# Top-256 selection: thresholds found by probing with false position and taking the eight largest of the rest, with the bitwise search kept behind a branch

## The chip, the cores and the metric

The kernel runs on one core of a Trainium2 chip. The core has a matrix engine (TensorE, PE in the profile), a vector engine (VectorE, DVE), a scalar engine (ScalarE, ACT), GpSimd (POOL) and a queue engine that issues the DMA transfers (SyncE, SP). Each works through its own instruction stream in order. The metric is the device time of one execution in microseconds (us); lower is better.

## The reference

Two transformer blocks run on a sequence of 2048 tokens of width 1024. The first block has two kinds of attention. The second projects its input, picks 256 keys for every query by an index score, attends to these alone, runs a gated recurrence (HGRN) beside it, and projects the sum. What the change touches is the picking:

```python
s_h = relu(einsum('bqhd,bkd->bqhk', qib, ki_r) * IDX_DIM**-0.5)     # 4 index heads
s_idx = einsum('bqhk,bqh->bqk', s_h, wib)
s_idx = where(key_pos[None, :] <= q_pos[:, None], s_idx, -inf)      # causal
_, sel = lax.top_k(s_idx, 256)                                      # per query row
# attention over the meta tokens and c_r[sel] only
```

So every query row needs the set of its 256 largest scores, ties going to the lowest key. Rows 0 to 255 have at most 256 keys and need no search. The other 1792 rows are 14 tiles of 128 rows; tile i (2 to 15) has 128(i+1) columns, 133 column blocks of 128 in all.

## The kernel before

The kernel is written with a scheduler that orders each engine's instructions ahead of time from priorities (the place in the program, moved by `high_priority`) and a model of durations; a loop in the source is unrolled, and work of later lines can be put into the gaps of earlier lines.

The program is `phase_first` (block one), `phase_proj2` (the projections of block two, index scores and selection) and `phase_dsa` (attention, HGRN, output). The change is in `phase_proj2` and behind `phase_dsa`.

In `phase_proj2`, `Index.scores` (L1457 to L1481) computes the scores of a tile: PE multiplies (L1469, L1470), ACT and DVE apply ReLU and the head weights (L1473 to L1477), POOL adds two halves (L1478), and SP stores the f32 scores to `d_sc`. `lat` computes latent keys and values. `stream` (L291) then runs twelve projection blocks: each loads 256 columns of weights, ACT, DVE and POOL scale and split them in two f16 halves (`load_w`, L255 to L277), and PE multiplies in three passes (`mm3_T`, L319 to L321, 512 columns an instruction; `mm3_R`, L330 to L332, 256 columns). ACT, and for some blocks DVE or POOL, takes the results out of PSUM, which gives PE its next bank.

`select` (L1500) finds for each row the 256th largest score as a 32-bit key, one bit a step, for a batch of tiles at once. It runs four times: tiles 2 to 7 beside 8 and 9 (pools `tk` and `ty`), and tiles 10 to 12 beside 13 to 15 (`tk` and `tk2`). Each of the 32 steps counts how many scores of each row lie at or above a candidate. `share` (L1484) splits a tile's columns for that: ACT counts some by a Sign with an accumulated sum on the f32 scores (L1553), DVE the others by a compare with an accumulated sum on 16-bit halves of the scores (L1545). About eight operations on one column per tile (L1538, L1539, L1577 to L1583) then set the next candidate. After the search each tile is turned into a mask of 0 and -1e30 (L1607 to L1623: Sign on ACT, a compare, a running count L1616 and a select L1620 on DVE, a subtraction on POOL, L1622 on DVE) and stored to `d_mask`, which `phase_dsa` reads. The mask stage of the second pair has its priority lowered by 800 (`LATE`).

Of the kernel before, what the change touches and what calls it, by code (L numbers as in the profile page):

```python
# [2 lines left out]

# [6 lines left out]
F32 = mybir.dt.float32  # L10
F32R = mybir.dt.float32r
BF = mybir.dt.bfloat16
F16 = mybir.dt.float16
I32 = mybir.dt.int32
U16 = mybir.dt.uint16
AF = mybir.ActivationFunctionType
ALU = mybir.AluOpType
AX = mybir.AxisListType
PSUM = bass.MemoryType.PSUM
DRAM = bass.MemoryType.DRAM  # L20

S = 2048
# [11 lines left out]
LATE = -800  # L34
# [39 lines left out]
PC, PO, NA, Z2 = -200, -1500, 5, 1  # L74
ACAP, DCAP = 9, 12
LEVELS = (1, 2, 4, 8, 16, 32, 64)
BATCHES = [((2, 3, 4, 5, 6, 7), (8, 9)), ((10, 11, 12), (13, 14, 15))]


def ap(t, off, pat):  # L80
# [1154 lines left out]
def phase_proj2(K, A, E, finish):  # L1235
    nc, tc = K.nc, K.tc
    K.wbufs, K.rbufs, K.wpool = 6, 4, WPOOL[1]
    with ExitStack() as st:
# [171 lines left out]
        finish(ps, "pp")  # L1410
        wp = st.enter_context(tc.tile_pool(name="w2", bufs=2, reuse_waits="tile"))
        tk = st.enter_context(tc.tile_pool(name="tk", bufs=1, reuse_waits="tile"))
        sy = st.enter_context(ExitStack())
        ty = sy.enter_context(tc.tile_pool(name="ty", bufs=1, reuse_waits="tile"))
        for g in range(NG):
            if g > 1:
                idx(g)
# [13 lines left out]
        blocks = [(*w2_of(A, cols), K.xinv, set2(kind, cols[0][0]), kind in ("ga", "gh")) for kind, cols in BLK2]  # L1431

        stream(K, wp, pst, [*blocks[:4], lambda: wo_scale(K, wp, pst, A["w_out_2"], "st"), *blocks[4:10], lambda: rel_rows(K, A, sp, pt, "pt0"), *blocks[10:]], "st")
        (x0, y0), (x1, y1) = BATCHES
        select(K, tk, x0, [x0, x1], 0)
        select(K, ty, y0, [y0], 0)
        sy.close()
        tk2 = st.enter_context(tc.tile_pool(name="tk2", bufs=1, side="right", reuse_waits="tile"))
        select(K, tk, x1, [x0, x1], LATE)
        select(K, tk2, y1, [y1], LATE)  # L1440
        with tc.high_priority(offset=-300):
            prod_scale(K, sp, pt, bd[:, :2], K.zm, K.as_, K.ainv, "pt0")

# [37 lines left out]
            nc.sync.dma_start(K.d_sc[i * 128:(i + 1) * 128, u * 512:u * 512 + w], acc)  # L1481


def share(tiles):  # L1484

    def parts(x):
        r = []
        for i in tiles:
            a = min(max(x, i + 1 - DCAP), i + 1, ACAP)
            r.append((a, i + 1 - a))  # L1490
            x -= a
        return r

    def cost(r):
        return max(sum(w * p[k] + f * (p[k] > 0) for p in r) for k, (w, f) in enumerate(COUNT))

    return min((parts(x) for x in range(sum(tiles) + len(tiles))), key=cost)


def select(K, tk, tiles, batches, late):  # L1500
# [105 lines left out]
    with K.tc.high_priority(offset=late):  # L1606
        for n, i in enumerate(tiles):  # L1607
            w = 128 * (i + 1)

            sn = junk("ja", w)  # L1610
            eq = junk("jd", w)
            pr = hflat[:, :w].bitcast(F16)
            c = cn[:, n:n + 1]
            nc.scalar.activation(sn, sc[n], AF.Sign, scale=-1.0, bias=fc[:, n:n + 1], accum_out=sg[:, n:n + 1])
            nc.vector.tensor_scalar(eq, sn, 0.0, None, op0=ALU.is_equal)
            nc.vector.tensor_tensor_scan(pr, eq, eq, 0.0, op0=ALU.add, op1=ALU.max)  # L1616

            nc.vector.tensor_tensor(c, sg[:, n:n + 1], pr[:, w - 1:w], op=ALU.add)
            nc.vector.tensor_scalar(c, c, 0.5, 256.0 - w / 2, op0=ALU.mult, op1=ALU.add)
            nc.vector.scalar_tensor_tensor(eq, pr, c, eq, op0=ALU.is_le, op1=ALU.mult)  # L1620
            nc.gpsimd.tensor_tensor(sn, sn, eq, op=ALU.subtract)
            nc.vector.tensor_scalar(sn, sn, -0.5, NEG, op0=ALU.is_gt, op1=ALU.mult)  # L1622
            nc.sync.dma_start(K.d_mask[i * 128:(i + 1) * 128, :w], sn)  # L1623


class Hgrn:
# [414 lines left out]
def build(tc, A, out):  # L2041
    nc = tc.nc
    with ExitStack() as ctx:
        K = Ctx()
        K.nc, K.tc, K.ctx = nc, tc, ctx
        consts(K)
        dp = ctx.enter_context(tc.tile_pool(name="dram", bufs=1, space=DRAM))
        for name, shape, dt in (
                ("d_q", [512, 2, S], F16), ("d_k", [512, 2, S], F16), ("d_kx", [8, 5, S], F16), ("d_qx", [1, 5, 512], F16),
                ("d_kc", [1, 2, NK], F16), ("d_z", [S, D], F32), ("d_qb", [512, 2, S], F16), ("d_kb", [128, 2, S], F16),  # L2050
                ("d_vf", [10, 128, NT, 129], F16),
                ("d_o", [S, D], F32), ("d_x1", [S, D], F32), ("d_qi", [256, 2, S], F16), ("d_ki", [64, 2, S], F16),
                ("d_q2", [512, 2, S], F16), ("d_k2", [512, 2, NK], F16),
                ("d_vf2", [8, 128, NT + 1, 129], F16), ("d_z2", [S, D], F32), ("d_f", [512, NK], F32),
                ("d_qh", [512, S], F32), ("d_i", [NK, 512], F32), ("d_sc", [S, S], F32), ("d_mask", [S, S], BF),
                ("d_rb", [2, 8, 512], F32), ("d_rbb", [8, 512], BF), ("d_cs", [2, 128, S], F32), ("d_gg", [1, D], F32), ("d_a", [S, D], F32)):
            setattr(K, name, dp.tile(shape, dt, name=name))
        with ExitStack() as sk:
            phase_proj2(K, A, *phase_first(K, A, sk))
        phase_dsa(K, A, out)  # L2060


def layout(i):
# [38 lines left out]
    for m in LEVELS:  # L2102
# [2 lines left out]
        s_ = np.arange(128)[:, None]  # L2105
        lv.append((s_ // (2 * m) == t // (2 * m)) & (s_ % (2 * m) < m))
    A["lvl"] = f(np.stack(lv, 1).astype(np.int32))
    p = np.arange(128)
    A["cum_l"] = ((p[:, None] % 8 == p[None, :] % 8) & (p[:, None] < p[None, :])).astype(np.float32)
    A["inv_freq"] = f(np.tile((10000.0 ** (-np.arange(32) / 32.0)).astype(np.float32), 4)[:, None])  # L2110
# [16 lines left out]
```

## Time and profile before

| | |
|---|---|
| time, median of 3 runs | 3434.53 us (3431.0 to 3434.55) |
| profiled execution | 3434.66 us; its span, first to last instruction, 3432.9 us |
| mean granted clock of TensorE | 0.915 of full |
| busy, share of span | PE 88%, DVE 72%, ACT 54%, POOL 41% |
| selection (first load of scores to last mask store) | 1496 to 2424 us of the span |

A profile is one execution. Busy time counts an engine's instructions and no waits; matmuls overlap in it, so a busy PE still has gaps. The trace can be asked for the busy time of each engine in a stretch, for groups of instructions by source line, for who waited for whom, and for instructions in order of time. A group's line gives the count, the busy time, the mean of one in ns, and behind the bar the idle time before them with what ended it.

### The profile page before, as it was taken

The numbers are of one execution on the slowest core, as the hardware profiler recorded it, in microseconds if no ns is written. First come the engines' busy times: TensorE is split into PE (matmuls) and PEld (weight loads), VectorE is DVE, ScalarE is ACT, GpSimd is POOL, SyncE is SP. The second block draws the span as 40 slices with busy tenths as digits, with TensorE's granted clock in tenths as the row PEclk, the third lists the DMA queues.
The fourth block names the chain that finished last, engine by engine and source line by source line (L and its number), as shares of the span: only waits on it lengthen the run. The fifth ranks groups of instructions, "written<-read, shape, count | busy, mean of one in ns | idle before, by whom it ended". The sixth has DMA issues, their size and how long they took to land. (4 is left out here: it accounts for less than half of the span.)

```text
span 3432.9 us, 67228 instructions
## 1 busy us (share of the span) xinstructions
PE 3006.7 (88%) x25150; PEld 1864.1 (54%) x25150; DVE 2480.9 (72%) x6097; ACT 1857.6 (54%) x3512; POOL 1415.0 (41%) x1235
## 2 busy tenths in 40 slices
PE   7899999999978998998878878787878898988997
PEld 5555444678844555443345753256555566555664
DVE  7423865666676766479999999995677778776654
ACT  4424755665565556345555576652555555555663
POOL 3212466643235454222233313122455556565653
PEclk9999999999968999998899888898678898999999
DMA  6332435322243432333234411113553443333332
GB/s 229 85 90 73 135 107 169 103 84 70 89 152 119 139 119 90 102 126 84 78 81 116 149 53 56 56 56 101 152 144 99 129 124 96 99 110 90 92 92 72
DMA packets 264288, 361.14 MB, mean 105 GB/s; under 512 B 55228, under 2 KB 185136, under 8 KB 262808
## 3 DMA queue, kind: packets, MB, share of 16 engines
q1 hardware_dynamic: 263528, 356.82, 34.5%
q8 instruction: 197, 3.23, 0.4%
q14 instruction: 131, 1.07, 0.1%
q10 hardware_dynamic: 432, 0.02, 0.0%
HBM read 243.92 MB, written 112.82 MB: 104 GB/s over the span
## 5 line engine op out<-in xcount | busy, mean ns | idle before, releaser
L746 POOL TENSOR_TENSOR plo<-p,phi 128x512 f16<-128x512 f32 (+4 forms) x628 | 680.4, 1095 | 710.7 <-ACT phi L742 444.9
L742 ACT CAST phi<-p 128x512 f16<-128x512 f32 (+4 forms) x681 | 366.7, 556 | 148.3 <-PE po L772 123.0
L1553 ACT ACTIVATE jk<-sc,fc 128x512 bf16<-128x512 f32 (+4 forms) x320 | 270.2, 844 | 244.9 <-DVE fc L1539 214.7
L740 ACT ACTIVATE p<-pst,shift,dci 128x512 f32<-128x512 f32 (+4 forms) x352 | 247.9, 717 | 146.8 <-PE pst L1928 56.9
L772 PE MATMUL po<-v,plo 128*128 128x65 f16 (+1 forms) x2304 | 286.4, 197 | 32.0 <-POOL plo L746 21.1
L770 PE MATMUL po<-v,phi 128*128 128x65 f16 (+1 forms) x2304 | 303.6, 198 | 6.6 <-ACT phi L742 5.6
L1873 DVE CUSTOM_DVE_ANT_0 jk<-p,mk 128x512 bf16<-128x512 f32 (+2 forms) x320 | 193.7, 605 | 153.8 <-PE p L1870 71.7
L771 PE MATMUL po<-v,phi 128*128 128x64 f16 (+1 forms) x2304 | 301.9, 199 | 0.0
L772 PEld LDWEIGHTS <-plo 128*128 128x128 f16 (+1 forms) x2552 | 247.2, 102 | 77.4 <-POOL plo L746 35.2
L956 DVE TENSOR_REDUCE mu<-p 128x1 f32<-128x512 f32 (+2 forms) x320 | 188.2, 603 | 124.7 <-PE p L952 81.9
L770 PEld LDWEIGHTS <-phi 128*128 128x128 f16 (+1 forms) x2552 | 248.0, 100 | 55.9 <-ACT phi L742 11.0
L740 ACT ACTIVATE p<-pst,shift,fci 128x512 f32<-128x512 f32 (+1 forms) x320 | 219.3, 710 | 103.4 <-PE pst L977 59.6
L277 POOL TENSOR_TENSOR wlo<-wraw,whi 128x512 f16<-128x512 f32 (+3 forms) x116 | 149.2, 1304 | 270.5 <-ACT whi L276 267.2
L771 PEld LDWEIGHTS <-phi 128*128 128x128 f16 (+1 forms) x2552 | 248.3, 100 | 13.5 <-issue 1.7
L330 PE MATMUL pp<-whi,hhi 128*128 128x256 f16 (+2 forms) x824 | 234.0, 285 | 8.0 <-ACT whi L276 5.7
L332 PE MATMUL pp<-whi,hlo 128*128 128x256 f16 (+2 forms) x824 | 232.0, 284 | 4.6 <-POOL hlo L458 4.6
L331 PE MATMUL pp<-wlo,hhi 128*128 128x256 f16 (+2 forms) x824 | 233.8, 284 | 0.6 <-POOL wlo L277 0.6
L1545 DVE TENSOR_SCALAR_CACHE_REDUCE jk<-hk,fc 128x1024 bf16<-128x1024 bf16 (+5 forms) x176 | 208.6, 1191 | 2.6
L1545 DVE TENSOR_SCALAR_CACHE_REDUCE jk<-hk,tl 128x1280 bf16<-128x1280 uint16 (+3 forms) x176 | 208.6, 1187 | 0.7
L319 PE MATMUL pp<-hhi,whi 128*128 128x512 f16 (+2 forms) x496 | 188.9, 381 | 7.1 <-DVE ra L516 4.4
L321 PE MATMUL pp<-hhi,wlo 128*128 128x512 f16 (+2 forms) x496 | 188.6, 381 | 0.0
L320 PE MATMUL pp<-hlo,whi 128*128 128x512 f16 (+2 forms) x496 | 188.5, 380 | 0.0
(638 smaller groups left out, 9110.9 us busy)
## 6 DMA issues: line engine op xcount, KB each, us to landing
wraw<-in_w_in_dram SPq DMA_DIRECT2D x88, 256.0 KB
d_z<-er SPq DMA_DIRECT2D x128, 128.0 KB
bT<-d_rb SPq DMA_DIRECT2D x32, 384.0 KB
wa<-in_w_ada_dram SPq DMA_DIRECT2D x8, 1024.0 KB
x<-in_x_dram SPq DMA_DIRECT2D x16, 512.0 KB
d_k<-ehi SPq DMA_DIRECT2D x32, 256.0 KB
d_q<-ehi SPq DMA_DIRECT2D x32, 256.0 KB
QA<-d_q SPq DMA_DIRECT2D x64, 128.0 KB
```

The costliest lines, as they stand in the source:

```text
L330: nc.tensor.matmul(ps, lhsT=hhi[:, kk, s], rhs=whi, start=kk == 0, stop=False)
L331: nc.tensor.matmul(ps, lhsT=hhi[:, kk, s], rhs=wlo, start=False, stop=False)
L332: nc.tensor.matmul(ps, lhsT=hlo[:, kk, s], rhs=whi, start=False, stop=kk == KK - 1)
L740: nc.scalar.activation(p, s, AF.Exp, scale=ci[:m], bias=K.shift[:m])
L742: nc.scalar.copy(hi, p)
L746: e.tensor_tensor(lo, p, hi, op=ALU.subtract)
L770: nc.tensor.matmul(o, lhsT=hi, rhs=v[:, :65], start=first, stop=False, **kw)
L771: nc.tensor.matmul(o[:, 1:65], lhsT=hi, rhs=v[:, 65:129], start=False, stop=False, **kw)
L772: nc.tensor.matmul(o, lhsT=lo, rhs=v[:, :65], start=False, stop=last, **kw)
L1545: nc.vector.tensor_scalar(junk("jd", x.shape[1]), x, t[:, n:n + 1], 0.0, op0=op, op1=ALU.add, accum_out=dst[:, n:n + 1])
L1553: nc.scalar.activation(junk("ja", a), sc[n][:, :a], AF.Sign, scale=-1.0, bias=fc[:, n:n + 1], accum_out=sg[:, n:n + 1])
L1873: nc.vector.tensor_tensor_reduce(jk[:, :w], p[:, :w], mk[s][:, u * 512:u * 512 + w], 1.0, 3.0 * NEG, op0=ALU.add, op1=ALU.max, accum_out=m ...
```

## The change

`select` is no longer called ahead of `phase_dsa`. A class `Quick` takes its place, run for tiles 2 to 9 and then 10 to 12 in pool `tk`, and 13 to 15 in `tk2`. All its counts read the f32 scores. Per batch it takes mean and deviation of the first 256 scores of each row, and makes two probes at plus and minus 1e-30 and eight more. A probe counts the scores above a candidate `t`, on ACT and DVE as before, with the columns split by other costs. The count is wanted near 252.5; a probe with 249 to 256 scores above it is kept in `R`. The next candidate is the false-position point of the bracket `B`, where an end that is kept twice has its value halved; the first two come from a normal quantile and one Newton step. Then the scores not above the kept probe are separated out, and the eight largest of them in each row give the exact threshold. The mask stage is the old one with two short operations more: they write `good` = 1 where the row's number of scores above its threshold and its number of ties admit exactly 256.

At the end of the program `count` adds up `good` over rows and tiles, every engine loads the number of rows that are not good, and if it is above zero, `select` runs for the four old batches, one after the other, and `phase_dsa` runs a second time.

```diff
-BATCHES = [((2, 3, 4, 5, 6, 7), (8, 9)), ((10, 11, 12), (13, 14, 15))]
+BATCHES = [(2, 3, 4, 5, 6, 7), (8, 9), (10, 11, 12), (13, 14, 15)]
+QUICK = [(2, 3, 4, 5, 6, 7, 8, 9), (10, 11, 12), (13, 14, 15)]
+PROBES = 8
+AIM = 252.5
+QCOST = ((106, 440), (150, 140))
...
-        (x0, y0), (x1, y1) = BATCHES
-        select(K, tk, x0, [x0, x1], 0)
-        select(K, ty, y0, [y0], 0)
-        sy.close()
+        K.quick.run(tk, QUICK[0], 0)
+        K.quick.run(tk, QUICK[1], LATE)
         tk2 = st.enter_context(tc.tile_pool(name="tk2", bufs=1, side="right", reuse_waits="tile"))
-        select(K, tk, x1, [x0, x1], LATE)
-        select(K, tk2, y1, [y1], LATE)
+        K.quick.run(tk2, QUICK[2], LATE)
...
+class Quick:
+    def run(self, tk, tiles, late):
...
+        parts = share(tiles, QCOST, 16, 16)
...
+        for n in range(nb):
+            nc.vector.bn_stats(bs[:, n], sc[n][:, :256])
+            nc.vector.bn_aggr(ag[:, n], bs[:, n])
...
+        def probe(t):
+            for n, p in enumerate(parts):
+                if p[0]:
+                    w = 128 * p[0]
+                    nc.scalar.activation(junk("ja", w), sc[n][:, :w], AF.Sign, scale=-1.0, bias=t[:, n:n + 1],
+                                         accum_out=sg[:, n:n + 1])
+            for n, p in enumerate(parts):
+                if p[1]:
+                    w = 128 * p[1]
+                    nc.vector.tensor_scalar(junk("jd", w), sc[n][:, 128 * p[0]:], t[:, n:n + 1], 0.0, op0=ALU.is_gt,
+                                            op1=ALU.add, accum_out=cn[:, n:n + 1])
+            nc.vector.scalar_tensor_tensor(u, cn, 2.0, sg, op0=ALU.mult, op1=ALU.subtract)
+            nc.vector.tensor_tensor(X[:, 1], u, lim, op=ALU.subtract)
...
+        def secant():
+            nc.vector.tensor_tensor(b, B[:, 0, 1], B[:, 1, 1], op=ALU.subtract)
+            nc.vector.reciprocal(b, b)
+            nc.vector.tensor_tensor(a, B[:, 1, 0], B[:, 0, 0], op=ALU.subtract)
+            nc.vector.tensor_tensor(b, b, B[:, 0, 1], op=ALU.mult)
+            nc.vector.tensor_tensor(a, a, b, op=ALU.mult)
+            nc.vector.tensor_tensor(X[:, 0], a, B[:, 0, 0], op=ALU.add)
...
+        for s in range(PROBES):
+            g, gp = G[s % 2], G[1 - s % 2]
+            probe(X[:, 0])
+            nc.vector.tensor_tensor(a, X[:, 1], X[:, 1], op=ALU.mult)
+            nc.vector.tensor_scalar(cv, a, (2 * (256 - AIM) + 0.5) ** 2, None, op0=ALU.is_le)
+            nc.vector.copy_predicated(R, cv[:, None, :].to_broadcast([128, 2, nb]), X)
+            if s == PROBES - 1:
+                break
...
+            end(0, g)
+            end(1, ng)
+            secant()
...
+        for n, i in enumerate(tiles):
+            w, c = 128 * (i + 1), 1024
+            ja = junk("ja", w)
+            nc.scalar.activation(ja, sc[n], AF.Relu, bias=T[:, n:n + 1])
+            for k, c0 in enumerate(range(0, w, c)):
+                x = slice(c0, min(w, c0 + c))
+                y = tk.tile([128, c], F32, name="y")[:, :x.stop - c0]
+                nc.vector.scalar_tensor_tensor(y, ja[:, x], -1e30, sc[n][:, x], op0=ALU.mult, op1=ALU.add)
+                nc.vector.max(top[:, n, 8 * k:8 * k + 8], y)
...
+        with K.tc.high_priority(offset=late):
...
+                nc.vector.tensor_tensor(gd, c, pr[:, w - 1:w], op=ALU.is_le)
+                nc.vector.scalar_tensor_tensor(gd, c, 0.0, gd, op0=ALU.is_ge, op1=ALU.mult)
...
+    def count(self, pool, pp):
...
+        nc.vector.tensor_reduce(s, self.good, axis=AX.X, op=ALU.add)
+        p = pp.tile([128, 512], F32, name="gp")
+        nc.tensor.matmul(p[:1, :1], lhsT=s, rhs=K.ones[:, :1], start=True, stop=True)
+        self.bad = pool.tile([1, 1], I32, name="bad")
+        nc.vector.tensor_scalar(self.bad, p[:1, :1], -1.0, 128.0 * (NT - 2), op0=ALU.mult, op1=ALU.add)
...
         phase_dsa(K, A, out)
+        with ExitStack() as st:
+            gp = st.enter_context(tc.tile_pool(name="gp", bufs=1, space=PSUM))
+            K.quick.count(qp, gp)
+        bad = nc.values_load(K.quick.bad[0:1, 0:1], min_val=0, max_val=S)
+        with tc.If(bad > 0):
+            with ExitStack() as st:
+                tk = st.enter_context(tc.tile_pool(name="tkg", bufs=1))
+                for b in BATCHES:
+                    select(K, tk, b, BATCHES, 0)
+            phase_dsa(K, A, out)
```

## Rows read from the trace of the kernel before

**Rows 1.** Busy time of each engine in four stretches: the selection, the attention phase behind it, and two stretches of block one. Columns: stretch in us, its length, then for PE, weight loads (PEld), DVE, ACT and POOL the busy time and the count, then granted TensorE clock, DMA share, GB/s.
```profile
1500.00:2410.00 910.00, 746.71 (x4384) 432.95 (x4382) 842.52 (x2289) 499.96 (x1108) 229.10 (x202) 0.88 0.28 85
2410.00:3433.00 1023.00, 893.62 (x9359) 581.64 (x9358) 714.52 (x1480) 554.81 (x909) 569.20 (x459) 0.89 0.38 108
750.00:950.00 200.00, 199.67 (x2281) 161.94 (x2278) 125.40 (x426) 116.72 (x223) 64.16 (x66) 1.00 0.26 79
200.00:300.00 100.00, 100.00 (x479) 46.25 (x478) 25.54 (x61) 28.18 (x55) 10.89 (x11) 1.00 0.30 94
```

**Rows 2.** Who waited for whom from 1500 to 2410 us. Columns: the waiting engine and line, the releaser, us in total, times, longest.
```profile
ACT jk L1553 <- DVE fc L1539: 214.7, 92, 8.3
POOL wlo L277 <- ACT whi L276: 181.9, 19, 36.2
POOL wrn L235 <- DVE wa L233: 73.0, 8, 17.4
PE psc L1469 <- DVE acc L1473: 29.3, 17, 4.5
PEld wsum L232 <- DVE wa L230: 29.0, 7, 7.7
```

**Rows 3.** The same stretch, busy time of single lines: in order L319, L330 and L1469 on PE (L320 and L321 count as L319, L331 and L332 as L330, L1470 as L1469), L1545 on DVE, L1553 on ACT.
```profile
1500.00:2410.00 910.00, 191.20 (x502) 51.89 (x501) 0.88 0.28 85
1500.00:2410.00 910.00, 223.04 (x784) 80.29 (x784) 0.88 0.28 85
1500.00:2410.00 910.00, 42.46 (x112) 11.73 (x112) 0.88 0.28 85
1500.00:2410.00 910.00, 430.26 (x726) 0.88 0.28 85
1500.00:2410.00 910.00, 296.34 (x640) 0.88 0.28 85
```

**Rows 4.** PE in order of time at full granted clock: 512 columns an instruction at 2201 us, 256 columns at 861 us. First column: start in us.
```profile
2201.15 0.38 PE L320 MATMUL st<-x1lo,whi 128*128 128x512 f16 x1
2201.37 0.38 PE L321 MATMUL st<-x1hi,wlo 128*128 128x512 f16 x1
...
861.12 0.27 PE L332 MATMUL pp<-whi,hlo 128*128 128x256 f16 x1
861.23 0.27 PE L330 MATMUL pp<-whi,hhi 128*128 128x256 f16 x1
```

**Rows 5.** DVE from 1500 to 2390 us, by line; those of the mask stage and of the search's small operations, and three counts and two two-input passes of known width.
```profile
L1616 DVE TENSOR_TENSOR_SCAN hk<-jk 128x384 f16<-128x384 bf16 (+13 forms) x14 | 38.1, 2725 | 0.2
L1620 DVE SCALAR_TENSOR_TENSOR jk<-hk,cn,jk 128x384 bf16<-128x384 f16 (+13 forms) x14 | 21.4, 1528 | 0.2
L1615 DVE TENSOR_SCALAR jk<-jk 128x384 bf16<-128x384 bf16 (+13 forms) x14 | 6.6, 471 | 12.1 <-ACT jk L1614 12.1
L1622 DVE TENSOR_SCALAR jk<-jk 128x384 bf16<-128x384 bf16 (+13 forms) x14 | 8.0, 569 | 11.9 <-POOL jk L1621 11.9
...
L1545 DVE TENSOR_SCALAR_CACHE_REDUCE jk<-hk,fc 128x1536 bf16<-128x1536 bf16 x32 | 57.7, 1809 | 0.3
L1598 DVE TENSOR_SCALAR_CACHE_REDUCE jk<-sc,fc 128x1536 bf16<-128x1536 f32 x1 | 1.8, 1803 | 0.0
L1598 DVE TENSOR_SCALAR_CACHE_REDUCE jk<-sc,fc 128x384 bf16<-128x384 f32 x1 | 0.6, 606 | 0.0
L1620 DVE SCALAR_TENSOR_TENSOR jk<-hk,cn,jk 128x1536 bf16<-128x1536 f16 x1 | 1.8, 1814 | 0.0
L1616 DVE TENSOR_TENSOR_SCAN hk<-jk 128x1536 f16<-128x1536 bf16 x1 | 3.4, 3350 | 0.0
```

**Rows 6.** DVE in order of time: two small operations that do not depend on one another, two that do, and a pass of statistics over 512 columns.
```profile
1661.98 0.16 DVE L1538 TENSOR_SCALAR tm<-T 128x2 int32<-128x2 int32 x1
1662.05 0.16 DVE L1577 TENSOR_SCALAR mm<-T 128x2 int32<-128x2 int32 x1
...
2334.69 0.17 DVE L1600 TENSOR_SCALAR sl<-cn 128x3 int32<-128x3 f32 x1
2334.89 0.17 DVE L1601 TENSOR_SCALAR sl<-sl 128x3 int32<-128x3 int32 x1
...
3424.73 0.69 DVE L1984 BATCH_NORM_STATS2 bs<-xr 128x6 f32<-128x512 f32 x1
```

**Rows 7.** ACT from 1500 to 2390 us, by line and shape: two widths of the count and the accumulator reads behind them.
```profile
L1553 ACT ACTIVATE jk<-sc,fc 128x1152 bf16<-128x1152 f32 x64 | 80.2, 1253 | 131.3 <-DVE fc L1539 126.7 <-DMA d_mask<-jk 2.4 <-DVE sl L1579 1.4
L1553 ACT ACTIVATE jk<-sc,fc 128x512 bf16<-128x512 f32 x96 | 68.6, 714 | 1.1
L1553 ACT ACTIVATION_READ_ACCUMULATOR jk<-sc,fc 128x1 f32 x320 | 60.0, 188 | 0.0
```

**Rows 8.** When the lines ran: the loads of scores into the searches (L1509), the first score operation on DVE (L1473), the running counts of the mask stage (L1616). Each gives minimum, median and maximum in ns and the first and last start in us.
```profile
L1509 SPq DMA_DIRECT2D sc<-d_sc x14: 319/423/525, 1495.9 to 1964.1; - x14
L1473 DVE TENSOR_SCALAR acc<-psc,wi x38: 339/742/751, 1413.0 to 1884.7; 128x512 f32<-128x512 f32 x28, 128x384 f32<-128x384 f32 x4, 128x128 f32<-128x128 f32 x3, 128x256 f32<-128x256 f32 x3
L1616 DVE TENSOR_TENSOR_SCAN hk<-jk x14: 945/2822/4425, 1828.4 to 2372.8; 128x384 f16<-128x384 bf16 x1, 128x512 f16<-128x512 bf16 x1, 128x640 f16<-128x640 bf16 x1, 128x768 f16<-128x768 bf16 x1
```

**Rows 9.** The end of the program in order of time: the last vector operation and the last issue of a DMA.
```profile
3427.80 1.28 DVE L1992 SCALAR_TENSOR_TENSOR xr<-xr,r,lbb 128x1024 f32<-128x1024 f32 x1
3429.11 0.33 SPq L1993 DMA_DIRECT2D out_dram<-xr  x1
```

More of the change, by code (lines that the diff above doesn't have):

```diff
@@ L1 @@
 import math
+from statistics import NormalDist
 from contextlib import ExitStack
@@ L76 @@
 LEVELS = (1, 2, 4, 8, 16, 32, 64)
-BATCHES = [((2, 3, 4, 5, 6, 7), (8, 9)), ((10, 11, 12), (13, 14, 15))]
+BATCHES = [(2, 3, 4, 5, 6, 7), (8, 9), (10, 11, 12), (13, 14, 15)]
+QUICK = [(2, 3, 4, 5, 6, 7, 8, 9), (10, 11, 12), (13, 14, 15)]
+PROBES = 8
+AIM = 252.5
+TINY = 1e-30
+QCOST = ((106, 440), (150, 140))
 def ap(t, off, pat):
@@ L1412, in phase_proj2 @@
         tk = st.enter_context(tc.tile_pool(name="tk", bufs=1, reuse_waits="tile"))
-        sy = st.enter_context(ExitStack())
-        ty = sy.enter_context(tc.tile_pool(name="ty", bufs=1, reuse_waits="tile"))
         for g in range(NG):
@@ L1481, in scores, with share @@
             nc.sync.dma_start(K.d_sc[i * 128:(i + 1) * 128, u * 512:u * 512 + w], acc)
-def share(tiles):
+def share(tiles, costs=COUNT, acap=ACAP, dcap=DCAP):
     def parts(x):
@@ L1488, in parts @@
         for i in tiles:
-            a = min(max(x, i + 1 - DCAP), i + 1, ACAP)
+            a = min(max(x, i + 1 - dcap), i + 1, acap)
             r.append((a, i + 1 - a))
@@ L1494, in cost @@
     def cost(r):
-        return max(sum(w * p[k] + f * (p[k] > 0) for p in r) for k, (w, f) in enumerate(COUNT))
+        return max(sum(w * p[k] + f * (p[k] > 0) for p in r) for k, (w, f) in enumerate(costs))
     return min((parts(x) for x in range(sum(tiles) + len(tiles))), key=cost)
@@ L2057, in build @@
             setattr(K, name, dp.tile(shape, dt, name=name))
+        qp = ctx.enter_context(tc.tile_pool(name="quick", bufs=1))
+        K.quick = Quick(K, A, qp)
         with ExitStack() as sk:
@@ L2107, in layout @@
     A["lvl"] = f(np.stack(lv, 1).astype(np.int32))
+    zq = np.zeros((3, NT - 2, 128), np.float32)
+    N = NormalDist()
+    for j in range((NT - 2) * 128):
+        n = 2 * 128 + j + 1
+        z = N.inv_cdf(1 - AIM / n)
+        zq[:, j // 128, j % 128] = 2 * (n - AIM), z, 1.15 / (2 * n * N.pdf(z))
+    A["zq"] = f(zq.transpose(2, 0, 1))
     p = np.arange(128)
```

104 lines of the change are left out of this document (added).

## The prediction

> **What bounds the kernel now.** I read the page's slices first (which engine is full where), then the busy times by stretch, then the lines and waits of the one stretch in which they stand out. The chain of waits is of no use here: its listed pieces lie in the attention phase, behind the change. From 1500 to 2410 us the vector engine is busy 842.5 of 910 us, 93%, while PE is busy 747 and its granted clock is 0.88 [rows 1]. In two stretches of block one the same kinds of projection run with PE busy to 100% at clock 1.00 (2.4 GHz): at 200 to 300 us with DVE at 26%, at 750 to 950 us with DVE at 63% and ACT at 58% [rows 1]. So DVE, not PE, sets the pace of the selection stretch, and it does so through its queue: ACT's counts wait 215 us for a new candidate from DVE, PE waits for the score operations (29 us) and for the sums that scale weights (29 us), and POOL's half of the weights stands behind ACT and DVE [rows 2]. The search is the reader's suspect because its counts alone hold DVE for 430 us [rows 3].
>
> **How much PE needs there.** Three lines of 502 instructions with 512 columns, three of 784 with 256, and two of 112 score multiplications [rows 3]. At full clock one of 512 columns follows the last by 0.215 us (2201.15 to 2201.37), one of 256 by 0.11 [rows 4]. That is 1506 x 0.215 = 324, 2352 x 0.11 = 259 and 224 x 0.215 = 48 us, 631 together; some 120 of the first are only 16 columns wide, some 300 other matmuls lie beside them, and I take 640 us. Of the 910 us, 270 are therefore PE's gaps and low clock. No change to the selection can give back more than that in this stretch, and the 1023 us of attention behind it have no selection in them [rows 1].
>
> **What the change removes.** On DVE, 32 counting steps of four batches: 430 us [rows 3]; about 900 small operations, at 0.07 us from start to start where they are independent [rows 6], 63 us; with the 16-bit copies, the splitting at bit 15 and the exact last count some 60 us more (an estimate: eleven tiles with three to four passes of about 1.3 us, as the 16-bit counts of such widths take [rows 5]). That is about 555. The mask stage stays: 38.1 + 21.4 + 6.6 + 8.0 = 74 us [rows 5]. So DVE's other work in the stretch is 842 - 555 - 74 = 213 us. On ACT, 296 us of counts with their reads go [rows 3].
>
> **What it adds, part by part.** Counts: the rule `share` with the new costs gives ACT 24, 19 and 24 column blocks of the three batches in 5, 2 and 2 instructions, DVE 28, 17 and 21 in 4, 2 and 2. An f32 count grows by (1803 - 606)/(1536 - 384) = 1.04 ns a column [rows 5], 0.133 us a block, with about 0.13 us fixed: 66 x 0.133 + 8 x 0.13 = 9.8 us a probe, and ten probes make 98 us. On ACT a column costs (1253 - 714)/640 = 0.84 ns, 0.108 us a block, and an instruction some 0.28 us and a read of 0.19 [rows 7]: 67 x 0.108 + 9 x 0.47 = 11.5, ten times 115 us. Small operations: I count some 180 a batch (18 in each middle probe), 540 in all, between 0.07 us each side by side and 0.20 us in a dependent row [rows 6], 38 to 108 us; 65 taken, since three batches give few neighbours. The eight largest: a pass of multiply and add over 17,024 columns and one of `max`; the nearest two-input pass of 1536 columns takes 1.81 us, the running count 3.35 [rows 5], so 18 + 18 to 18 + 37 us and some 7 us fixed; 45 taken, by the first row. ACT's ReLU over them is 133 x 0.108 + 14 x 0.28 = 18 us. Statistics over 256 columns, 14 times: half of 0.69 us and one small operation [rows 6], 8 us. `good` adds 28 small operations, 4 us. The mask stage repeats its 74. DVE then holds 213 + 98 + 65 + 45 + 8 + 4 + 74 = 507 us of work (475 to 570), ACT 500 - 296 + 115 + 18 = 337. POOL's load stays.
>
> A rule of the Trainium skill speaks against the switch of the counts to f32. The rows first: a count of 1536 columns takes 1809 ns on bf16 and 1803 ns on f32 [rows 5], no difference. The Trainium skill, page "VectorE: DVE Perf Modes", section "The perf-mode tier table", gives such scalar operations on bf16 twice the rate of fp32; by that ratio the new counts would be 196 us and DVE's load 605. The measurement decides here, and even by the Trainium skill's ratio DVE would stay under PE's 640.
>
> **What is late next.** PE. With DVE at 507 and ACT at 337 over some 700 us, both are at shares (72% and 48%) close to those of the stretch at 750 to 950 us, where PE had no gap [rows 1]. The selection itself is a dependent chain: a probe takes the longer of the two counts (4.9, 3.0 and 3.5 us on ACT) and some 18 small operations in a row at 0.2 us, 8.5, 6.6 and 7.1 us; ten probes, the eight largest and the masks make about 150, 115 and 130 us of each batch alone. The second batch takes the score buffer of the first in `tk`, so its loads wait in SP's queue until the first batch's masks are done, and stores behind them in that queue wait too; the third has its own pool. The scores now come from 1413 to 1885 us and the last search is loaded at 1964 [rows 8]; even with the first batch from 1560 us, all three one after the other end at 1560 + 395 = 1955, before the projections could. So this chain is hidden; if the stream's operations doubled it, it would end near 2350 and be the bound (second rival). The later masks keep their lowered priority; their waits for ACT and POOL hold nothing that PE needs first, and rows 0 to 511 of the attention need tiles 2 and 3 only.
>
> PE will not reach 640. Score and latent work with short results, and the start of the attention, leave gaps. At 92% I get 696 us, a gain of 214. The bounds: 98% gives 653 and a gain of 257; a gap loss left half as large as today's (135 of 270 us) gives 775 and 135.
>
> **The branch.** It lies behind everything: a sum, a matmul, a small operation, a register load on every engine, a compare. No row shows a load of this kind or a branch. From below it is near nothing, if the sum is done while the last store lands (3429.1 to the end at 3432.9 us [rows 9]). From above I take eight such round trips of 3.8 us, 30 us; I take three, 11 us, and with the three small steps 12. The Trainium skill, page "Runtime: NRT & Kernel Launch", section "Instruction fetch mechanics", says that a taken branch to code outside the fetched window stalls until that code has been loaded; no run here shows it, and the code to be jumped over is a second attention phase long.
>
> **Sum.** 3434.66 - 214 + 12 = 3233 us against the profiled execution. Its time is 0.1 us from the median of the runs shown, so I carry it over unchanged: 3233.
>
> **The rivals.** First, *half the gain*: PE stays coupled to in-order queues. A count of 16 blocks blocks DVE for 2.2 us and ACT's for 1.8, and what takes a result out of PSUM stands behind it. For it speaks that the waits on ACT and DVE in [rows 2] are waits in a queue, not for long work; against it that 750 to 950 us ran dense at similar shares. Half of the gap remains: 3434.7 - 135 + 12 = 3312. A *selection chain that ends last* gives much the same: an end at 2350 instead of 2410 us plus the branch, 3387; the dense PE needs no more than 1500 + 696 by then. Second, *the whole gap goes*: 3434.7 - 257 + 5 = 3183. For it speaks the 100% of 200 to 300 us; against it the 26% DVE load there.
>
> On the other side, *the branch is taken*. One row among 1792 whose eight probes all miss the band of eight counts is enough. Its price: the four old searches alone, DVE's 555 us with the masks' 74, then the attention again, 1023 us [rows 1]: 3233 + 1650 = 4885 us, slower. For it speaks that nothing in the method bounds the number of misses, and that scores built from ReLUs have a lump at zero and are not normal. Against it: both sides of zero are probed first, the start is within some tens of counts, and in a bracket of twenty counts a linear guess should err by a few, so each later probe hits more often than not; the loss of six in a row is rare, but 1792 rows draw. Whether the change does what it says is this same question.
>
> **How the numbers follow.** Forecast 58%, half the gain 18%, chain last 4%, the whole gap 12%, branch taken 7%, no gain because something unseen eats it 1%. The forecast's own range is 3195 to 3275 (DVE 475 to 570, branch 0 to 30, gaps 5 to 12%). The range that holds eight in ten takes in the whole gap below and most of the half gain above: 3175 to 3330; the branch lies outside. Faster by over 0.2%, about what a measurement of this kernel tells from no change: 0.92; within: 0.01; slower: 0.07.
>
> **What would show it.** Right: in the profile after, the projections end near 2200 us, PE busy above 90% in that stretch at a clock near 0.95 or more, DVE at 65 to 80%, the wait of ACT's counts for the candidate far under 215 us, counts on DVE near 98 us in 80 instructions, and nothing of L1500's search. The last mask store lies well before the last projection. Behind the last output there are some 10 us of short operations. Wrong: DVE still above 90%, or PE's gaps now released by ACT; the masks ending last; a span with two attention phases; or attention behind 1023 us by more than 20, which no step here foresees.

## The result, and the profile after

The changed kernel takes 3275.37 us (median of 4 runs, 3273.87 to 3276.06) against 3433.27 us for the kernel before in the same comparison. The ratio is 0.954, with a 95% interval from 0.9524 to 0.9557: 158 us are gone. The forecast was 3233 us, a gain of 202; the time lies inside the range of 3175 to 3330 and 42 us above the forecast. The profiled execution took 3274.8 us, its span is 3272.7 us.

The first view is the busy time by stretch, cut where the last projection matmul starts: at 2387.78 us before and at 2249.49 us after (read from PE's rows in order of time). Columns as in [rows 1]: the stretch, its length, then busy time and count of PE, weight loads, DVE, ACT and POOL, then granted clock, DMA share and GB/s. First the kernel before, cut in this way:

```profile
1500.00:2387.80 887.80, 735.13 (x4328) 427.03 (x4327) 835.92 (x2251) 494.64 (x1100) 228.97 (x201) 0.89 0.27 83
2387.80:3432.90 1045.10, 905.20 (x9417) 587.56 (x9414) 721.12 (x1518) 560.14 (x916) 569.33 (x459) 0.88 0.38 110
```

Then the kernel after:

```profile
1500.00:2249.50 749.50, 697.60 (x4355) 416.83 (x4355) 500.58 (x1306) 345.62 (x670) 251.22 (x214) 0.95 0.33 103
2249.50:3272.70 1023.20, 887.42 (x9419) 581.71 (x9416) 722.62 (x1508) 558.23 (x916) 564.55 (x454) 0.89 0.38 110
```

The selection stretch has become 138 us shorter, the attention behind it 22 us. DVE falls from 94% of the stretch to 67%, PE rises from 83% to 93% and its clock from 0.89 to 0.95. Of the attention's 22 us I make little: in the profiled executions of the runs below, where the same attention code follows, it takes from 1010 (no_branch) to 1037 us (no_selection), and the 1045 before lie 8 us above that. The forecast has them in its gain all the same, because its stretch of 910 us ends 22 us behind the start of the last projection.

The second view is the waits from 1500 to 2250 us, which answers to [rows 2], cut to the lines that answer to those rows and to what the text below names (waiting line, releaser, us in total, times, longest):

```profile
POOL wlo L284 <- ACT whi L283: 127.9, 19, 34.1
...
ACT wjk L262 <- DMA wraw<-in_w_in_dram: 48.3, 21, 9.0
...
ACT whi L283 <- DVE wraw L282: 34.5, 11, 11.2
...
ACT jk L1786 <- DMA d_mask<-jk: 24.7, 5, 9.2
...
ACT jk L1694 <- DVE X L1720: 11.8, 9, 2.9
PEld wsum L239 <- DVE wa L237: 11.7, 6, 5.8
...
PE pp L328 <- POOL wlo L284: 8.3, 2, 6.1
...
ACT jk L1694 <- DVE X L1712: 6.8, 3, 3.9
...
ACT jk L1694 <- DVE X L1724: 6.4, 1, 6.4
...
PE psc L1471 <- DVE acc L1475: 3.3, 4, 1.3
```

ACT's counts (L1694) waited 215 us for a new candidate in the kernel before [rows 2]; now its waits for one (the three rows with X) come to 25 us. PE's wait for the score operations is down from 29 to 3 us, the weight loads' wait for the weights' sums (PEld wsum) from 29 to 12, and POOL's wait for ACT's half of the weights from 182 to 128. What is left sits in the preparation of weights (L262, L283, L284) and in the mask stage (L1786).

The third view says where in time. Windows of 50 us, same columns:

```profile
1850.00:1900.00 50.00, 37.99 (x318) 32.36 (x317) 43.31 (x125) 29.55 (x53) 19.48 (x19) 0.90 0.46 166
...
1950.00:2000.00 50.00, 50.00 (x283) 27.50 (x282) 47.27 (x160) 34.79 (x54) 17.39 (x10) 1.00 0.19 65
2000.00:2050.00 50.00, 42.33 (x184) 18.41 (x183) 45.84 (x55) 17.79 (x28) 38.68 (x15) 0.93 0.20 69
2050.00:2100.00 50.00, 34.42 (x141) 14.34 (x140) 36.56 (x49) 11.89 (x20) 29.41 (x17) 0.83 0.34 112
2100.00:2150.00 50.00, 50.00 (x235) 22.87 (x234) 12.54 (x28) 13.35 (x25) 5.39 (x5) 1.00 0.26 89
```

PE is full at clock 1.00 from 1950 to 2000 us, while the search of the last two batches holds DVE at 95%. It starves from 2000 to 2100 us, when the masks of tiles 10 to 15 are made: 23 of 100 us are gaps, and the clock falls to 0.83. A second hole, 12 us, lies at 1850 to 1900 us; it is there in no_late_masks below too (13.8 us of gaps in the same window), and no run here explains it. The last mask store is issued at 2088.0 us.

The last view is DVE's lines from 1500 to 2250 us, those that the prediction costed (busy time, and behind the comma the mean of one in ns):

```profile
L1699 DVE TENSOR_SCALAR_CACHE_REDUCE jk<-sc,X 128x128 bf16<-128x128 f32 (+5 forms) x80 | 104.1, 1306 | 0.5
L1788 DVE TENSOR_TENSOR_SCAN y<-jk 128x384 f16<-128x384 bf16 (+13 forms) x14 | 38.8, 2774 | 0.2
L1767 DVE SCALAR_TENSOR_TENSOR y<-jk,sc 128x1024 f32<-128x1024 bf16 (+7 forms) x22 | 23.7, 1080 | 1.8 <-ACT jk L1763 1.6
L1794 DVE SCALAR_TENSOR_TENSOR jk<-y,cn,jk 128x384 bf16<-128x384 f16 (+13 forms) x14 | 22.6, 1612 | 0.0
L1768 DVE MAX8 top<-y 128x8 f32<-128x1024 f32 (+7 forms) x22 | 21.0, 957 | 0.2
L1796 DVE TENSOR_SCALAR jk<-jk 128x384 bf16<-128x384 bf16 (+13 forms) x14 | 13.8, 989 | 7.7 <-POOL jk L1795 7.7
L1787 DVE TENSOR_SCALAR jk<-jk 128x384 bf16<-128x384 bf16 (+13 forms) x14 | 10.6, 757 | 15.8 <-ACT jk L1786 15.8
L1793 DVE SCALAR_TENSOR_TENSOR good<-cn,good 128x1 f32<-128x1 f32 x14 | 9.3, 663 | 0.0
L1792 DVE TENSOR_TENSOR good<-cn,y 128x1 f32<-128x1 f32 x14 | 7.0, 496 | 0.2
```

Counts 104 us in 80 instructions, the eight largest 44.7 us in two lines (L1767, L1768), the masks 85.8 in four (L1787, L1788, L1794, L1796). DVE's whole load, 500.6 us, stands at the 507 that the working gave, ACT's 345.6 at 337.

### The profile page after: what moved, and what is told of

It is laid out like the page before. It is cut to its first block, busy times and chain, and to the rows that moved or that the text cites. A ratio compares the mean times of both kernels' runs of the same rounds, so it can differ in the third digit from the quotient of the medians.

```text
span 3272.7 us, 65807 instructions
## 1 busy us (share of the span) xinstructions
PE 2951.4 (90%) x25152; PEld 1846.6 (56%) x25152; DVE 2132.7 (65%) x5113; ACT 1698.7 (52%) x3066; POOL 1430.2 (44%) x1239
## 5 line engine op out<-in xcount | busy, mean ns | idle before, releaser
L753 POOL TENSOR_TENSOR plo<-p,phi 128x512 f16<-128x512 f32 (+4 forms) x628 | 689.0, 1109 | 729.8 <-ACT phi L749 439.3
L779 PE MATMUL po<-v,plo 128*128 128x65 f16 (+1 forms) x2304 | 283.1, 196 | 16.1 <-POOL plo L753 12.5
L284 POOL TENSOR_TENSOR wlo<-wraw,whi 128x512 f16<-128x512 f32 (+3 forms) x116 | 151.2, 1320 | 238.5 <-ACT whi L283 211.6
L778 PEld LDWEIGHTS <-phi 128*128 128x128 f16 (+1 forms) x2552 | 246.6, 100 | 13.8 <-issue 2.9
L328 PEld LDWEIGHTS <-wlo 128*128 128x128 f16 (+2 forms) x1000 | 99.8, 100 | 123.1 <-issue 12.2
L326 PEld LDWEIGHTS <-whi 128*128 128x128 f16 (+2 forms) x1000 | 100.2, 101 | 118.7 <-issue 13.6
L327 PEld LDWEIGHTS <-whi 128*128 128x128 f16 (+2 forms) x1000 | 100.0, 101 | 114.8 <-issue 16.7
```

The source lines that it names most:

```text
L326: nc.tensor.matmul(ps, lhsT=whi, rhs=hhi[:, kk, :], start=kk == 0, stop=False)
L327: nc.tensor.matmul(ps, lhsT=whi, rhs=hlo[:, kk, :], start=False, stop=False)
L328: nc.tensor.matmul(ps, lhsT=wlo, rhs=hhi[:, kk, :], start=False, stop=kk == KK - 1)
L753: e.tensor_tensor(lo, p, hi, op=ALU.subtract)
L778: nc.tensor.matmul(o[:, 1:65], lhsT=hi, rhs=v[:, 65:129], start=False, stop=False, **kw)
L779: nc.tensor.matmul(o, lhsT=lo, rhs=v[:, :65], start=False, stop=last, **kw)
```

## The experiments

The question is where the 42 us stayed. The first four runs leave out or double a part.

**no_selection** leaves the whole selection out: zeros are stored as masks, and every row counts as good.

```diff
+        zt = tk.tile([128, wide], BF, name="zt")
+        nc.vector.memset(zt, 0.0)
+        nc.vector.memset(self.good[:, cols], 1.0)
+        for i in tiles:
+            nc.sync.dma_start(K.d_mask[i * 128:(i + 1) * 128, :128 * (i + 1)], zt[:, :128 * (i + 1)])
+        return
```

> Leaves out the whole selection: no scores loaded, no probes, no eight largest, no mask stage; zero masks are stored and good is set to 1, so the branch stays and is not taken. Theory A (what is left of the selection still costs PE: in the changed kernel the stretch from 1500 us to the end of the projections takes 752 us where PE needs 640): the stretch comes down to 640/0.96 = 667, time 3275 - 85 = 3190 us. Rival B (the rest is scores, latents and weights, not the selection): 3240 us or more.

Measured: 3235.75 us, ratio 0.9399 (0.9351 to 0.9446), so 48 us less than the change by the ratios' difference (0.0141 x 3434; with the two intervals, some 30 to 65). That is nearer to rival B than to theory A. The last projection starts at 2197.29 us:

```profile
1500.00:2197.30 697.30, 680.45 (x4359) 412.30 (x4359) 191.06 (x418) 218.40 (x452) 185.34 (x197) 0.98 0.33 98
```

This is the reading that settles the miss. With no selection at all, PE is busy 680 of 697 us: 97.6% at clock 0.98. The work itself needs close to 680 us, not the 640 that the prediction took. Even without any selection the projections end at 2197 us, where the forecast put them with one (1500 + 696). Of the 749.5 us after, 680 are need, 17 more busy time at the lower clock, and 52 gaps.

**no_branch** takes the count, the register loads, the branch and the code behind it away.

```diff
-            K.quick.count(qp, gp)
-        bad = nc.values_load(K.quick.bad[0:1, 0:1], min_val=0, max_val=S)
-        with tc.If(bad > 0):
...
```

> Leaves out the sum of good, the register load, the branch and the code behind it; the rest is the changed kernel. By the trace after, the last output issue to the end takes 6.0 us where it took 3.8 before: 2 to 3 us less, 3272.5 us. By the prediction's term, 12 us less, 3263 us.

Measured: 3282.54 us, ratio 0.9545 (0.9505 to 0.9585): no difference that can be measured. The trace resolves more than the times here. The last store is issued at

```profile
3266.74 0.33 SPq L2178 DMA_DIRECT2D out_dram<-xr  x1
```

in the kernel after, 6.0 us before the end of its span, and in no_branch at

```profile
3264.12 0.33 SPq L2178 DMA_DIRECT2D out_dram<-xr  x1
```

3.8 us before the end (3267.9), as in the kernel before [rows 9]. At the end of the program the branch costs 2.2 us. The matmul of the count runs at 3185 us already, beside other work, since all rows' `good` are known by 2080 us.

**probes_16** doubles the probes from eight to sixteen.

```diff
-PROBES = 8
+PROBES = 16
```

> Sixteen probes where there were eight, nothing else. Eight more probes add 78 us of counts and some 30 us of small operations to DVE and 92 us to ACT. Theory A (DVE and ACT have room, PE sets the pace): at most 40 us more, 3275 to 3315 us. Rival (the selection's chain or DVE's queue sets the end): 8 x (8.5 + 7.1) = 125 us more, 3400 us.

Measured: 3286.05 us, ratio 0.9547 (0.9507 to 0.9587). Eight more probes put 84 us on DVE's counts and cost nothing that can be measured:

```profile
L1699 DVE TENSOR_SCALAR_CACHE_REDUCE jk<-sc,X 128x1280 bf16<-128x1280 f32 (+7 forms) x144 | 188.2, 1308 | 1.9
```

The last projection starts at 2256.30 us, 7 us later than after the change. So neither DVE's load nor the length of the search holds PE, as theory A has it. The chain's room is used up by it, though: the last mask store moves from 2088.0 to 2278.9 us, 22 us behind the start of the last projection. With eight probes the selection ends 161 us ahead of it, so it is not what ends last.

**no_late_masks** leaves out the mask stage of tiles 10 to 15; zeros are stored for them.

```diff
+        if late:
+            zt = tk.tile([128, wide], BF, name="jk", tag="ja")
+            nc.vector.memset(zt, 0.0)
...
+            return
         with K.tc.high_priority(offset=late):
```

> Leaves out the mask stage of tiles 10 to 15 alone: their searches run, zero masks are stored, good is 1. Theory A (these masks, 2000 to 2090 us, hold back the weights of the next projection blocks, and PE is busy 77 of 100 us there): 25 to 40 us less, 3235 to 3250 us. Rival B (the weights are late by themselves): 0 to 8 us less, 3267 us or more.

Measured: 3246.4 us, ratio 0.9422 (0.9382 to 0.9462), 40 us under the change by the ratios (some 25 to 55 with the two intervals), as theory A has it. The window in which PE starved is nearly full:

```profile
2000.00:2050.00 50.00, 48.00 (x224) 21.52 (x223) 21.02 (x52) 15.96 (x26) 26.97 (x23) 1.00 0.45 159
2050.00:2100.00 50.00, 50.00 (x236) 23.02 (x235) 11.48 (x28) 13.30 (x26) 8.10 (x8) 1.00 0.24 80
```

So of what the selection still costs, most comes from six tiles' masks: 40 of 48 us by the times, neither known to better than some 15. The two profiles show less, the last projection 24 us earlier (2225.08) where no_selection has it 52 us earlier, and an attention 5 us longer than the change's; this profile is of the slowest of the four executions.

The next runs ask what in the mask stage does it. ACT's Sign (L1786) writes one buffer, from which the mask is stored in the end, so the next tile's Sign waits for that store; the squares and copies of weights stand behind it in ACT's queue. That is one theory (A). The other (B) is the length of the mask's own operations on DVE and POOL, ahead of the weights' operations in their queues. The changed kernel ran along as a yardstick (**after_again**, no edit).

> The changed kernel once more, as the yardstick for the three runs beside it. Its ratio to the kernel before was 0.954 (0.9524 to 0.9557); expected 0.952 to 0.957 again, the last projection near 2250 us.

Measured: 3286.45 us, ratio 0.9553 (0.9523 to 0.9583). The last projection starts at 2249.71 us.

**inplace** writes the mask, and the scratch row `eq` beside it, into the place of the tile's own scores:

```diff
-                eq = junk("jd", w)
+                mk, eq = (sc[n].bitcast(BF)[:, k * w:(k + 1) * w] for k in range(2))
...
-                nc.gpsimd.tensor_tensor(sn, sn, eq, op=ALU.subtract)
-                nc.vector.tensor_scalar(sn, sn, -0.5, NEG, op0=ALU.is_gt, op1=ALU.mult)
+                nc.gpsimd.tensor_tensor(mk, sn, eq, op=ALU.subtract)
+                nc.vector.tensor_scalar(mk, mk, -0.5, NEG, op0=ALU.is_gt, op1=ALU.mult)
-                nc.sync.dma_start(K.d_mask[i * 128:(i + 1) * 128, :w], sn)
+                nc.sync.dma_start(K.d_mask[i * 128:(i + 1) * 128, :w], mk)
```

> The mask of a tile is written into the place of its own scores, which nobody reads any more, so that the Sign of the next tile on ACT no longer waits for the mask's store. Theory A: the 30 to 40 us that the late masks cost come from the single buffer: the Sign waits for the store (some 33 us of ACT's waits from 2000 to 2110 us, releaser DMA of d_mask), and the squares and copies of weights stand behind it in ACT's queue. Then the wait falls to under 10 us, PE from 2000 to 2100 us rises from 77 to over 90 us, and the time falls by 15 to 35 us against after_again (ratio 0.944 to 0.950). Theory B: they come from the length of the mask's own operations on DVE and POOL; then the wait is gone but the time stays within 8 us.

Measured: 3284.75 us, ratio 0.9548 (0.9518 to 0.9579), the same as the yardstick. The wait for the store is gone, and others have its place (waits from 2000 to 2110 us, the Sign's own):

```profile
ACT jk L1786 <- POOL sc L1795: 11.0, 2, 7.1
ACT jk L1786 <- DVE nt L1777: 10.9, 1, 10.9
```

ACT's Sign now waits for the subtraction on POOL and for the threshold. Theory A falls. Its estimate of the wait was too high as well: the yardstick's row from 2000 to 2110 us says 19.1 us, not 33.

**no_pool** takes the subtraction off POOL; the mask is where (rank above c) + sign exceeds 0.5:

```diff
-                nc.vector.scalar_tensor_tensor(eq, pr, c, eq, op0=ALU.is_le, op1=ALU.mult)
-                nc.gpsimd.tensor_tensor(sn, sn, eq, op=ALU.subtract)
-                nc.vector.tensor_scalar(sn, sn, -0.5, NEG, op0=ALU.is_gt, op1=ALU.mult)
+                nc.vector.scalar_tensor_tensor(sn, pr, c, sn, op0=ALU.is_gt, op1=ALU.add)
+                nc.vector.tensor_scalar(sn, sn, 0.5, NEG, op0=ALU.is_gt, op1=ALU.mult)
```

> The subtraction on POOL leaves the mask stage: the mask is (rank above c) + sign > 0.5, in the two DVE operations that stood around it. The buffers stay. Theory A (the single buffer): the Sign's wait for the store stays, the time changes by under 8 us. Theory B (the operations): POOL is some 30 us less busy, the wait of SP's queue for POOL's e (46 us) falls under 20, and the time falls by 10 to 30 us.

Measured: 3270.28 us, ratio 0.9499 (0.9476 to 0.9521), 18 us under the yardstick (0.0054 x 3434), with intervals that do not meet. POOL is 37 us less busy from 1500 to 2250 us (252.65 to 215.47). Part of theory B's signature failed, though. SP's waits from 1985 to 2100 us in the yardstick:

```profile
SPq L1387 <- POOL e L1386: 46.5, 13, 7.5
SPq L1797 <- DVE jk L1796: 15.8, 3, 7.8
SPq L1797 <- DVE wa L240: 11.8, 1, 11.8
...
SPq L1797 <- DVE cn L1791: 6.6, 1, 6.6
```

and in no_pool, where the mask store is L1796:

```profile
SPq L1387 <- POOL e L1386: 46.3, 11, 10.7
...
SPq L1796 <- DVE jk L1795: 14.2, 4, 6.6
...
SPq L1796 <- DVE wa L240: 1.7, 1, 1.7
```

The wait for POOL's `e` did not fall; it was SP's wait in front of the mask stores that fell, from 34 to 16 us. In the profiled execution, which is the slowest of the six, the last projection starts only 5 us earlier (2244.50).

There is a second thing that the waits don't list, because it lies inside DVE's own instructions. In the kernel after, DVE and POOL in order of time:

```profile
2074.07 4.05 DVE L1792 TENSOR_TENSOR good<-cn,y 128x1 f32<-128x1 f32 x1
...
2080.23 3.70 DVE L1796 TENSOR_SCALAR jk<-jk 128x2048 bf16<-128x2048 bf16 x1
```

```profile
2074.05 4.05 POOL L1795 TENSOR_TENSOR jk<-jk 128x2048 bf16<-128x2048 bf16 x1 [2.23 <-DVE cn L1791]
2080.05 3.32 POOL L1795 TENSOR_TENSOR jk<-jk 128x1664 bf16<-128x1664 bf16 x1 [1.96 <-DVE good L1793]
```

A DVE operation on one column, 0.16 us in the median of its 14, lasts 4.05 us and ends with POOL's subtraction; a one-input pass over 2048 columns, 0.69 us in the kernel before, lasts 3.70 and ends 0.6 us behind POOL's. Two more of the late masks' operations do the same (L1793 at 2014.50 us, L1787 at 2045.34): the four take 14 us where 1.6 would do. In no_pool the subtraction is gone, and the same four operations take 2.0 us together. So DVE stood still for some 12 us in POOL's subtractions (why the two engines end together, the rows do not tell). How the 18 us divide between this and SP's shorter wait is not shown.

**inplace_no_pool** makes both edits (`eq` stays in its own buffer).

> Both edits. Theory A: as inplace, within 8 us. Theory B: as no_pool. If each holds a part: 20 to 40 us under after_again, near the ratio of the kernel without late masks, 0.942.

Measured: 3264.72 us, ratio 0.9489 (0.9458 to 0.9521); the last projection starts at 2238.46 us. That is 22 us under the yardstick, and its interval lies nearly on no_pool's; the place of the mask adds nothing that can be told apart. Run again as **both_again**:

> The kernel of inplace_no_pool once more, as the yardstick for masks_act_queue. Its ratio to the kernel before was 0.949 (0.946 to 0.952); if the gain over the change (0.954 to 0.955) is real, the interval stays under 0.9525 again.

Measured: 3271.05 us, ratio 0.9501 (0.9475 to 0.9527). The intervals of both runs lie below the yardstick's or touch its lower end: some 17 us (0.5%) less than the change, for the same masks. The profiles agree: in the four without POOL's subtraction (these, no_pool and the next run) the last projection starts at 2232 to 2244.5 us, in the five that have it and all eight probes and masks (the change, after_again, inplace, no_branch, forced) at 2249 to 2258. Of the 40 us of the late masks, some two fifths can be had so.

**masks_act_queue** issues the mask stores from ACT's queue instead of SP's:

```diff
-                nc.sync.dma_start(K.d_mask[i * 128:(i + 1) * 128, :w], mk)
+                nc.scalar.dma_start(K.d_mask[i * 128:(i + 1) * 128, :w], mk)
```

> As both_again, but the mask stores are issued from ACT's queue and not from SP's. Theory: the rest of the loss from 2000 to 2100 us is SP's queue, where loads of weights stand behind mask stores that wait for DVE (ACT's squares waited 16 us for weights there). Then these waits fall under 5 us, PE from 2000 to 2100 us rises from 86 to over 93 us and the time falls by 5 to 15 us against both_again. Rival: ACT's own copies and squares now stand behind the store that waits for DVE; then the time is equal or up to 15 us longer.

Measured: 3273.85 us, ratio 0.9509 (0.9483 to 0.9536), the same as both_again. ACT's squares still wait 15.2 us for weights (16.1 in both_again), and PE from 2000 to 2100 us is busy 87.4 us (86.5). The mask stores in SP's queue were not what held the weights' loads. What holds PE for the rest of what the late masks cost, 20 us or so, stays open.

**forced** raises the number of rows not good by one, so that the branch is always taken:

```diff
-        nc.vector.tensor_scalar(self.bad, p[:1, :1], -1.0, 128.0 * (NT - 2), op0=ALU.mult, op1=ALU.add)
+        nc.vector.tensor_scalar(self.bad, p[:1, :1], -1.0, 128.0 * (NT - 2) + 1.0, op0=ALU.mult, op1=ALU.add)
```

> The number of rows not good is raised by one, so that the branch is always taken and the old search and a second attention phase run: the price of one row that the probes miss. From the change's own time of 3275: plus the prediction's 1650 us (DVE's 555 and 74 us of search and masks, 1023 us of attention) gives 4925. If the four searches, which now have nothing beside them and run one after the other, are paced by their dependent chains rather than by DVE's work, the search part is 750 to 1000 us and the time 5050 to 5300. Beyond either, the load of the code jumped to would show in the gap between the branch and the first instruction behind it.

Measured: 5124.06 us in one run, 1849 us over the change. The searches and masks run from 3274 to 4159 us, 885 us, and the attention from there to 5122, 963 us. The second case of the expectation has the number, its reason only in part:

```profile
3280.00:4080.00 800.00, 56.17 (x492) 49.15 (x492) 709.05 (x1889) 336.03 (x681) 77.62 (x47) 0.51 0.10 33
```

and DVE's two costliest groups in it:

```profile
L1547 DVE TENSOR_SCALAR_CACHE_REDUCE jk<-hk,fc 128x1280 bf16<-128x1280 bf16 (+3 forms) x176 | 209.9, 1192 | 5.1
L1547 DVE TENSOR_SCALAR_CACHE_REDUCE jk<-hk,tl 128x1280 bf16<-128x1280 uint16 (+3 forms) x164 | 193.2, 1178 | 3.7
```

DVE is busy 709 of 800 us, so its own work is most of the length, and waits are some 11%. The counts (L1547) are 403 us of that work; the six small operations that every step has (L1540, L1541, L1579 to L1582) add 132, at 0.16 to 0.20 us each, where the prediction had put all small operations at 63 us. The 56 us of PE are work of the second attention that has been drawn forward, and DVE has a part of it too. The jump itself, DVE first and SP behind it in order of time:

```profile
3272.66 1.28 DVE L2177 SCALAR_TENSOR_TENSOR xr<-xr,r,lbb 128x1024 f32<-128x1024 f32 x1
3273.89 0.06 DVE L1532 MEMSET lim<- 128x1 f32 x1
```

```profile
3273.97 0.33 SPq L2178 DMA_DIRECT2D out_dram<-xr  x1
3274.46 3.28 SPq L1511 DMA_DIRECT2D sc<-d_sc  x6
```

DVE's first instruction behind the branch (L1532) starts within the last one ahead of it, and SP's follows 0.5 us after the last store's issue. The rule of the Trainium skill that the prediction named (page "Runtime: NRT & Kernel Launch", section "Instruction fetch mechanics": a taken branch to code outside the fetched window waits for that code) has no gap to show for it on these two engines; how long before the last vector operation the branch was decided, the rows do not tell.

## Why the prediction was right and where it missed

- **DVE's queue bounds the stretch before: right.** With the search replaced, ACT's wait for the candidate falls from 215 to 25 us and DVE from 94% to 67%, and the projections end 138 us earlier.
- **"I take 640 us" for PE's need: wrong, and this is the step that failed.** no_selection shows 680. Its distances from one start to the next, idle time left out, divide them so: 306.7 us for the projection instructions with 512 columns and their short ones (300 worked out), 262.0 for those with 256 (259), 72.6 for the score multiplications (48), and 39.1 for the some 250 others (latents, weight sums, transposes), where the step left 33 (640 less 631, plus the 24 us by which the 16-column ones are shorter). The score multiplications are most of the miss: they go at 0.31 us, not 0.215, as this pair of no_selection shows (first column the start):

```profile
1654.63 0.38 PE L1471 MATMUL psc<-KI,QI 128*128 128x512 f16 x1
1654.94 0.39 PE L1472 MATMUL psc<-KI,QL 64*128 64x512 f16 x1
```

  The kernel before has the same distance in its own trace (granted clock 1.00 from 1560 to 1575 us), so that the term could have been read there:

```profile
1569.63 0.38 PE L1469 MATMUL psc<-KI,QI 128*128 128x512 f16 x1
1569.94 0.39 PE L1470 MATMUL psc<-KI,QL 64*128 64x512 f16 x1
```

  By the median distance of each kind of instruction in the trace before, the same work comes to 669 us (an estimate), and by those of no_selection to 668; the 12 us from there to 680 fit its clock of 0.98 (680 x 0.02 is 14). So the gap that a change could give back was some 230 us of the 910, not 270.
- **How the 42 us come about.** The projections end 53.5 us later than 1500 + 696: 40 are the need, and 13 are gaps and low clock (69 us where 56 were allowed). The branch gave back 10 (2.2 us where 12 stood), the attention 2. That the attention fits is luck: the forecast took it as the 1023 us behind 2410, where from the start of the last projection it had been 1045, and no step says why it should come down to the 1021 that it took.
- **Density 92%: nearly right**, 680 of 749.5 us, 91%. But the reason given for the remaining gaps (score and latent work, the start of the attention) is the smaller part: no_selection has those and stands at 97.6%. The larger part is the mask stage, of tiles 10 to 15 above all, which the prediction let pass with "hold nothing that PE needs first". It does hold something: 40 us by the times of no_late_masks, 24 in its profile. Which operation of the weights' preparation it holds was not isolated.
- **DVE's 507 and ACT's 337 us: right**, 501 and 346, DVE's in part by luck. Counts took 104 for 98 (and 6.5 of reads), the eight largest 44.7 for 45. The masks took 86 for 74 and `good` 16 for 4, the long ones among them held by POOL as shown at no_pool (the median of L1792 is 0.16 us, of L1793 0.15). Against that, DVE's other work came to some 175 us where the working had 213 (each instruction counted up to the start of the next). probes_16 shows that even 84 us more would have stayed hidden.
- **Chain hidden: right, but longer than worked out**: the last mask store is at 2088 us, 161 before the last projection and 133 behind the 1955 of the working, though the third batch was searched beside the second.
- **Branch 12 us: right in place, too dear**, 2.2 us. The count could be worked out long before the end, so of the steps listed at most the loads and the compare were left. The price of taking it was set at 1650 and is 1849: search and masks, 629 us of DVE by the step, last 885 (small operations at 0.16 to 0.20 us and not 0.07, and waits), and the attention 963 instead of 1023, some of it done beside the search.
- **Rivals.** Half the gain (3312) and the whole gap (3183) bracket the result; the first's mechanism, a coupling through in-order queues, is likely the one in the mask stage (no run separates it from DVE's stops in POOL's subtractions), the second was out of reach at a need of 680 us. No row missed, since the branch wasn't taken.

## What to carry to other kernels

Before a gap is put down as gain, find what the work needs without it: add up the distances from start to start for every line of the stretch, small ones too, or time the kernel with the work left out. 84 us more of counts on DVE were free, while the masks of six tiles (50 us on DVE) cost 40: a busy time alone does not tell what work costs. That it is the other work standing behind it in the queues at that moment is the reading that fits; the runs show the two costs and not the reason. Compare the longest instruction of a group with the median, too: one on a single column that lasts 4 us has stood still for something. A fallback behind a branch that isn't taken cost 2 us where its condition is known early; its price when taken is the serial one, 885 us here where the work of the parts that it repeats had been put at 629.

## What the runs showed that was not expected

- Two score matmuls of 512 columns, with 128 and 64 rows of contraction, follow one another at 0.31 us at a granted clock of 1.00 in their window, while projections of the same width go at 0.215 [rows 4]. Unequal rows alone don't do it: in the attention of the kernel after, a pair with 66 and 128 rows (L2101, L2102, from 3183.70 us, granted clock 1.00) follows at 0.23 and 0.22 us.
- DVE operations can last until a two-input operation of POOL ends: one on a single column took 4.05 us beside POOL's subtraction, and 0.16 in the median.
- With the projections denser, PE's clock rises from 0.89 to 0.95 and, with no selection, to 0.98, both near its upper level (2.4 GHz); the 50-us window with the lowest clock between 1500 and 2250 us, 0.83, is the one with the most gaps (PE busy 34.42).
- A kernel with the same attention code had it take 1010 to 1037 us in different profiled executions, so a change of 15 us there isn't to be read from one profile.
